# A feed forward in one unit: Strassen's product in both projections, and the samples as a stream of their own

## The chip, the core and the metric

The kernel runs on one core of one Trainium2 chip. The metric is the time of one execution on the device in microseconds (us), lower is better. The engines run side by side and wait for one another by semaphores: PE (TensorE) multiplies matrices, DVE (VectorE), ACT (ScalarE) and POOL (GpSimd) work on elements, and SP (SyncE) issues the transfers between the chip's memory (DRAM) and the core's own memory (SBUF). A matmul's result is in PSUM, a small memory of eight banks.

## What is computed

One layer of a streaming encoder in fp32, for 1024 tokens of a prompt and 8 samples of 16 tokens. These are nine tiles of 128 tokens, of 1024 features each.

```python
z = x @ w_in                         # recurrence (HGRN2) and sliding window attention
x = LN(ALPHA * x + concat(A, B) @ w_out)
x = LN(ALPHA * x + memory_attention(x) @ w_mo)
x = LN(ALPHA * x + (silu(x @ w_gate) * (x @ w_up)) @ w_down)    # d_ff = 2816
```

The last line is the feed forward, of which the change speaks. In the kernel `w_f1` holds gate and up weights and `w_f2` the down weights, both laid out in advance in the blocks that the kernel loads.

## The kernel before

An exact fp32 product is expensive on PE. So most operands are split in two parts in a faster format (`split`, L132 and L133): ACT casts the upper part `w_hi`, and DVE subtracts it from the source to get the remainder `w_lo`. A product is then three matmuls (hi·hi, lo·hi, hi·lo), `mm3`. All matmuls of a line L93 come from one helper, transposes from L97; in the changed kernel these are L95 and L99, and `split` is L137 and L138. The group column of the profile therefore names the tiles.

Two stages precede the feed forward. Stage 1 (`phase1`) projects the inputs and does both kinds of attention; its last work is the memory's keys and values (`mem_kv`), whose results go to the output and to a scratch by way of the tile `kv_sb`. Stage 2 takes the tokens in three groups of three tiles: output projection (`w_out`), layer norm, memory attention, and its projection (`mem_out`, weights `w_mo`). The rows that leave it are stored to `x2_scratch` (`x_scratch` in the profile). The samples' tile is the third of the nine.

The feed forward before runs in two units, of four and of five tiles; the samples are in the first one.

- `unit_operands` transposes a unit's rows and forms the seven operands `B11`, `T1`, `T2`, `B22`, `T3`, `B21`, `T4` of Strassen's product in Winograd's form (on ACT, POOL and DVE), each split in two.
- `hidden` makes two feature tiles, a pair, of which there are 11: it loads four weight tiles, forms the sums `s1` to `s4` on POOL and DVE, and does seven products instead of eight, each 2 × 4 × 3 matmuls, with 256 columns in the first unit and 320 in the second. Then follow tanh and two products for the gate, and the split of `h`.
- `ffn` takes a few pairs (a part), then their second projection (`proj_rows`, 512 columns, plain, three matmuls per product), and adds the result to the rows (`add_rows`, L705). With the last part come layer norm and the store.

The order on each engine comes from streams of emission, ranked, with an estimated clock (`Order`), and each engine runs its list in that order. All loads stand in one list on SP. A load stands there until its buffer is free, and all that is behind it in the list waits with it. Raw weights have three buffers (`raw_tile`), split weights four pairs.

Of the kernel before, what the change touches and what calls it, by code (L numbers as in the profile page):

```python
# [35 lines left out]
# tokens go in the order of ORDER: two tiles of the prompt, the samples (tile 8), the other tiles of the prompt  # L36
# [6 lines left out]
class Event:  # L43
    """a point on TensorE's clock from which a result is expected to be there"""
# [34 lines left out]
class TensorE:  # L79
    """TensorE with the products' cost added to the clock of an Order"""  # L80
# [19 lines left out]
def trunk(ctx, tc, I, O):  # L100
# [10 lines left out]
    wp = pool("wp")  # L111
# [6 lines left out]
    def bank(name):  # L118
        return pp[name][0].tile([P, 512], F32, name=name, bufs=pp[name][1])
# [41 lines left out]
    class Quads(list):  # L161
        """feature-major blocks [P, GW] in two parts, four to a slot"""
# [40 lines left out]
    def fm(wsrc, x, which="a", n=GW, w=None):  # L203
        """one block of columns, feature major"""
# [9 lines left out]
    ident = const.tile([P, P], F32, name="ident")  # L214
    make_identity(nc, ident)
    tri = const.tile([P, 640], U8, name="tri")
    own = const.tile([P, 8], F32, name="own")
    sinks = const.tile([P, 8], F32, name="sinks")
    sinks_s = const.tile([P, 2], F32, name="sinks_s")
    gnorm = const.tile([P, P], F32, name="gnorm")  # L220
# [3 lines left out]
    carry = const.tile([P, HGH, P], F32, name="carry")  # L224
    V.memset(carry, 0.0)
    starts = [const.tile([P, GW], F32, name=f"starts{i}") for i in range(2)]
# [142 lines left out]
    def hgrn(g, h, xt, tm):  # L369
# [53 lines left out]
        def body():  # L423
# [14 lines left out]
            # from chunks to pairs of chunks  # L438
# [45 lines left out]
    def hgrn_sample(h, qg, kdt, v, at, pl, po, sv):  # L484
        """the sample's tile: a chunk and a state for each of its sequences"""
# [25 lines left out]
    def finish(sb, mx, sk, nk):  # L511
        """rows of sb [P, n, .]: exp(s - max), normalised with the sink's share"""
# [12 lines left out]
    def swa_tile(p1, ip, t, pos, q, ak, av):  # L525
        """heads 2 ip and 2 ip + 1 of both groups, one tile of queries over its own and the preceding tile of keys"""
# [105 lines left out]
    def proj_rows(src, wsrc, evac, which, ahead=(), nt=GT, by_tile=False):  # L632
        """rows of nt tiles; src: blocks [P, nt * P] in two parts"""
# [205 lines left out]
    def mem_sample(p2, qf, ot, ready):  # L839
# [5 lines left out]
        def cache():  # L845
            """the next part of the caches, four sequences to a tile"""
# [55 lines left out]
    class Unit:  # L902
        def __init__(self, t0, nt, pieces, tmp, row, th):
            self.t0, self.nt, self.n = t0, nt, nt * 64
            self.pieces, self.tmp, self.row, self.th = pieces, tmp, row, th
            self.ready = Event()

        def operand(self, op, kt):
            for k0, hi, lo in self.pieces[op]:
                if k0 <= kt < k0 + hi.shape[1]:  # L910
                    return hi[:, kt - k0], lo[:, kt - k0]

    def unit_operands(u):
# [6 lines left out]
        for t in range(u.nt):  # L920
            b = {}
            for q in range(2):
# [4 lines left out]
                for e in range(2):  # L927
                    b[f"B{q + 1}{e + 1}"] = v[:, :, e]
# [215 lines left out]
    def wait(e):  # L1144
        yield e
# [114 lines left out]
```

## Time and profile before

| what | us |
|---|---|
| three runs | 1668.59, 1675.08, 1677.58 |
| median | 1675.08 |
| span of the profiled execution | 1669.8 |
| PE, busy | 1618.8 (97%) |
| DVE, busy | 1235.5 (74%) |
| ACT, busy | 735.8 (44%) |
| POOL, busy | 244.2 (15%) |
| DMA, mean rate | 140 GB/s |

The profile is of one execution, of which the profiler gives the span. A row of a timeline has the start in us from the span's start, the duration, the engine (SPq is SP's queue of transfers), the line, the operation, the tiles as out<-in, the count, and in brackets the idle time before it with what ended it. A row of a group ends with the count, the busy time, the mean duration of one in ns, the idle time before, and what it waited for. A DMA row has the count, the size of one, and the median time from issue to landing. Matmuls are pipelined, so their pitch, from one start to the next, is what counts, and not the duration of one.

### The profile page before, as it was taken

The page shows a single profiled execution, that of the slowest core. Times are in us where ns is not written, and L with a number is a line of the kernel's source. Part 1 is how long each engine was busy: PE and PEld are TensorE (multiplying, and loading weights), DVE is VectorE, ACT ScalarE, POOL GpSimd, SP SyncE. Part 2 cuts the span into 40 slices and gives each one's busy share as a digit, 9 for nine tenths or more (in the row PEclk, how much of TensorE's full clock was granted, in tenths as well). Part 3 has the DMA queues.
Part 4 walks back from the last instruction along what each step waited for, and adds up shares of the span by engine and source line. Part 5 has one row for each costly group of instructions (what it writes and reads, how often), then busy time and mean ns, then how long its engine had stood idle before and what let it go on. Part 6 is the DMA issues. An engine that isn't in the chain of part 4 may idle for free. (4 is left out here: it accounts for less than half of the span.)

```text
span 1669.8 us, 26720 instructions
## 1 busy us (share of the span) xinstructions
PE 1618.8 (97%) x10341; PEld 1477.3 (88%) x10341; DVE 1235.5 (74%) x2161; ACT 735.8 (44%) x1471; POOL 244.2 (15%) x234
## 2 busy tenths in 40 slices
PE   8999999999999999999988999999989999999998
PEld 7998999999878987879878898989888999989896
DVE  6887688788568666787799577667898757566568
ACT  4543455445543555224645244345543424334241
POOL 1111121111000000000232110212232111111111
PEclk9999999999999999999999999999999999999999
DMA  7453343333884588646332523132543313131231
GB/s 244 128 179 125 93 151 102 105 115 108 277 313 149 169 274 311 234 138 227 101 114 91 176 89 127 64 101 91 175 168 122 101 58 107 51 101 64 89 100 65
DMA packets 84800, 233.65 MB, mean 140 GB/s; under 512 B 10048, under 2 KB 28352, under 8 KB 84672
## 3 DMA queue, kind: packets, MB, share of 16 engines
q1 hardware_dynamic: 84672, 231.93, 42.4%
q8 instruction: 81, 1.33, 0.3%
q14 instruction: 47, 0.39, 0.1%
HBM read 210.86 MB, written 20.97 MB: 139 GB/s over the span
## 5 line engine op out<-in xcount | busy, mean ns | idle before, releaser
L133 DVE TENSOR_TENSOR w_lo<-w_raw,w_hi 128x1024 fp32r<-128x1024 f32 (+1 forms) x279 | 343.1, 1232 | 166.4 <-ACT w_hi L132 165.5
L132 ACT CAST w_hi<-w_raw 128x1024 fp32r<-128x1024 f32 (+1 forms) x279 | 290.0, 1041 | 323.8 <-PE a L93 147.0
L93 PE MATMUL a<-w_hi,h 128*128 128x512 f32 x756 | 242.6, 394 | 5.2 <-DVE rows L705 2.6
L93 PE MATMUL a<-w_hi,q_hi 128*128 128x256 f32 (+1 forms) x576 | 197.0, 344 | 3.5 <-ACT w_hi L132 2.9
L93 PE MATMUL a<-w_lo,q_hi 128*128 128x256 f32 (+1 forms) x576 | 197.0, 342 | 1.9 <-DVE w_lo L133 1.8
L93 PE MATMUL a<-w_hi,q_lo 128*128 128x256 f32 (+1 forms) x576 | 195.4, 339 | 0.0
L93 PE MATMUL a<-q_hi,w_hi 128*128 128x384 f32 x528 | 186.8, 354 | 6.8 <-ACT q_hi L132 4.3
L93 PE MATMUL a<-q_hi,w_lo 128*128 128x384 f32 x528 | 180.1, 341 | 0.0
L93 PE MATMUL a<-q_lo,w_hi 128*128 128x384 f32 x528 | 179.9, 341 | 0.0
L93 PEld LDWEIGHTS a<-w_hi,h 128*128 128x128 f32 x756 | 141.8, 188 | 38.5 <-ACT h L1000 3.6
L132 ACT CAST w_hi<-w_s 128x1024 fp32r<-128x1024 f32 x88 | 92.2, 1048 | 181.3 <-PE a L93 87.9
L133 DVE TENSOR_TENSOR w_lo<-w_s,w_hi 128x1024 fp32r<-128x1024 f32 x88 | 134.6, 1533 | 35.9 <-ACT w_hi L132 35.9
L93 PE MATMUL a<-w_lo,h 128*128 128x512 f32 x378 | 148.2, 392 | 0.0
L970 POOL TENSOR_TENSOR w_s<-w_raw 128x1024 f32<-128x1024 f32 x22 | 54.8, 2492 | 490.6 <-DMA w_raw<-in_w_f_dram 428.7
L93 PE MATMUL a<-x,w_hi 128*128 128x256 f32 x704 | 126.3, 280 | 0.0
L93 PEld LDWEIGHTS a<-w_hi,q_hi 128*128 128x128 f32 x576 | 108.5, 188 | 17.9 <-ACT w_hi L132 3.3
L705 DVE SCALAR_TENSOR_TENSOR rows<-rows,a 128x512 f32<-128x512 f32 x123 | 82.7, 682 | 55.6 <-PE a L93 55.4
L93 PEld LDWEIGHTS a<-w_lo,q_hi 128*128 128x128 f32 x576 | 108.6, 189 | 16.8 <-DVE w_lo L133 3.4
L93 PEld LDWEIGHTS a<-w_hi,q_lo 128*128 128x128 f32 x576 | 108.6, 188 | 12.7 <-issue 0.5
L93 PEld LDWEIGHTS a<-q_hi,w_hi 128*128 128x128 f32 x528 | 100.6, 191 | 11.7 <-ACT q_hi L132 4.4
L93 PEld LDWEIGHTS a<-x,w_hi 128*128 128x128 f32 x704 | 108.1, 188 | 0.3
L93 PEld LDWEIGHTS a<-q_lo,w_hi 128*128 128x128 f32 x528 | 100.8, 191 | 1.9 <-issue 0.9
(247 smaller groups left out, 3662.5 us busy)
## 6 DMA issues: line engine op xcount, KB each, us to landing
w_raw<-in_w_f_dram SPq DMA_DIRECT2D x110, 512.0 KB, 3.6
w_raw<-in_w_fm_dram SPq DMA_DIRECT2D x41, 512.0 KB, 4.1
w_raw<-in_w_tm_dram SPq DMA_DIRECT2D x24, 512.0 KB, 3.6
w_raw<-in_w_out_dram SPq DMA_DIRECT2D x24, 512.0 KB, 5.4
w_raw<-in_w_mq_dram SPq DMA_DIRECT2D x24, 512.0 KB, 4.4
w_raw<-in_w_mo_dram SPq DMA_DIRECT2D x24, 512.0 KB, 4.1
w_s<-in_w_f_dram SPq DMA_DIRECT2D x22, 512.0 KB, 4.4
ln_gb<-in_ln_dram SPq DMA_DIRECT2D x16, 512.0 KB, 6.7
```

Of the source, the lines that this page charges most:

```text
L93: return self.eng.matmul(out, lhsT, rhs, **kw)
L132: S.copy(hi, src)
L133: V.tensor_tensor(lo, src, hi.bitcast(F32), op=ALU.subtract)
L705: V.scalar_tensor_tensor(y[t][:, hs], y[t][:, hs], scale, ps, op0=ALU.mult, op1=ALU.add)
L970: G.tensor_tensor(s1, a21, a22, op=ALU.add)
```

## The change

The prompt's eight tiles are now one unit. Every hidden product has 512 columns, so each weight of `w_f1` is loaded and split once instead of twice. `h` is not kept but stored to `h_scratch` in DRAM.

The second projection now uses Strassen's product too (`second_projection`): 4 blocks of two tiles, 11 pairs in parts of 3, 3, 3 and 2. For a part, `prepare` loads `w_f2`, forms the sums of weights on POOL and splits all four tiles per pair; `inputs` loads `h` of one block, forms its sums on POOL and splits seven operands; `block` does the seven products.

The samples' first projection (`sample_hidden`) is no longer part of a unit: it multiplies plain fp32, unsplit weights `w_s` with `xs`, the transposed samples, in 22 half steps of 16 matmuls, as the stream `filler` of the lowest rank. Each half step needs two tiles of `w_f1`, so that these weights are loaded a second time. The products of the samples' second projection stand among those of the parts.

The pools of SBUF are cut anew: constants of stage 1 and the stage's right side are closed when they are done, and the feed forward opens `c` (operands), `f1` (hidden) and `f2` (second projection) in their place.

The diff, cut to what the text speaks of:

```diff
-UNITS = ((0, 4, ((0, 6), (6, 12), (12, 16), (16, 22))),
-         (4, 5, ((0, 2), (2, 6), (6, 10), (10, 14), (14, 18), (18, 22))))
+TILES = (0, 1, 3, 4, 5, 6, 7, 8)
+SAMPLE = 2
+PAIRS = FT // 2
+PARTS = ((0, 3), (3, 6), (6, 9), (9, 11))
...
+    def sample_hidden(i):
+        ps = bank("b")
+        for e in range(2):
+            w = []
+            for q in range(2):
+                w.append(ff["sample_w"]())
+                nc.sync.dma_start(out=w[q], in_=I["w_f1"][i, e * 2 + q])
+            for z in range(2):
+                for kt in range(KT):
+                    T.matmul(ps[:, cols(e * 2 + z)], w[kt // 4][:, cols(z * 4 + kt % 4)], xs[:, kt],
+                             start=kt == 0, stop=kt == KT - 1)
+            if e == 0:
+                yield
...
+        a11, a21, a22, a12 = wt("a11", 0), wt("a21", 2), wt("a22", 3), wt("a12", 1)
+        s1, s2, s4 = wt("s1"), wt("s2"), wt("s4")
+        G.tensor_tensor(s1, a21, a22, op=ALU.add)
+        G.tensor_tensor(s2, s1, a11, op=ALU.subtract)
+        G.tensor_tensor(a21, a11, a21, op=ALU.subtract)
+        G.tensor_tensor(s4, a12, s2, op=ALU.subtract)
...
+        def prepare(i):
+            w0, w1, s12, s34 = (f2.tile([P, 1024], F32, name=x, tag="w", bufs=5) for x in ("w0", "w1", "s12", "s34"))
+            for n, t in enumerate((w0, w1)):
+                nc.sync.dma_start(out=t, in_=I["w_f2"][n, i])
...
+            for t, x in ((w0, "w0"), (s12, "s12"), (s34, "s34"), (w1, "w1")):
+                out.append(parts_of(t, *(f2.tile([P, 1024], F32R, name=x + y, bufs=3) for y in "hl")))
...
+    def feed_forward(rows):
+        right.close()
...
+        ff["sample_w"] = raw_tile
...
+        order.add(all_operands(ops, rows, ready), 6)
+        order.add(filler(), 10)
+        yield ready
+        left.close()
...
+        for i in range(PAIRS):
+            yield from hidden(f1, ops, i)
+        cs.close()
+        fs.close()
+        psums.close()
...
+        ff["sample_w"] = lambda: f2.tile([P, 1024], F32, name="w_s", tag="w", bufs=5)
+        yield from second_projection(f2)
```

Three places of the order show what moved. In its rows, `[waits ...]` names the engines or queues whose semaphores the row waits for (DMAHW for earlier transfers), and xN counts equal rows.

**SP, where stage 1 ends.** Before, the first load for the output projection, `w_raw` from `w_out`, stood ahead of the stores of the last memory values:

```order
L143 DMA w_raw_5704<-in_w_mv_dram 128x1024 [waits DMAHW6_49,DVE_49]
L143 DMA w_raw_5751<-in_w_out_dram 128x1024 [waits DMAHW1_49,DVE_49]
L199 DMA raw_5640<-mix_scratch 128x384 [waits DMAHW7_49,DMAHW2_49,DVE_49]
L199 DMA raw_5644<-mix_scratch 128x384 [waits DMAHW3_49,DMAHW0_49,DVE_49]
L264 DMA out_2_dram<-kv_sb_5602 128x512 [waits Activation_49]
L266 DMA mem_kv_scratch<-kv_sb_5602 128x256 x2
L264 DMA out_2_dram<-kv_sb_5607 128x512 [waits DMAHW4_49,Activation_49]
```

Now the tiles of stage 2 and its constants come first, then the stores of the last values, which wait for ACT's copies, and behind them the first `w_out` load:

```order
L719 DMA rows_5795<-in_xtok_dram 128x1024 [waits DMAHW0_49,PE_49]
L689 DMA ln_gb_5823<-in_ln_dram 128x1024 [waits DMAHW1_49,PE_49]
L689 DMA ln_gb_5825<-in_ln_dram 128x1024 [waits DMAHW2_49]
L269 DMA out_2_dram<-kv_sb_5725 128x512 [waits DMAHW3_49,Activation_49]
L271 DMA mem_kv_scratch<-kv_sb_5725 128x256 [waits DMAHW4_49]
L271 DMA mem_kv_scratch<-kv_sb_5725 128x256 [waits DMAHW5_49]
L269 DMA out_2_dram<-kv_sb_5730 128x512 [waits DMAHW6_49,Activation_49]
L271 DMA mem_kv_scratch<-kv_sb_5730 128x256 [waits DMAHW7_49]
L271 DMA mem_kv_scratch<-kv_sb_5730 128x256 [waits DMAHW0_49]
L148 DMA w_raw_5763<-in_w_out_dram 128x1024 [waits DMAHW1_49]
```

What moved is the first `w_out` load, to a place behind two waits for ACT.

**PE, where stage 2 ends.** Before, the last product of `mem_out` (with `q`, the attention's output) was followed by the first hidden product (`x2`, the operand `B11`):

```order
L93 MATMUL a_9578<-w_hi_9520,q_lo_8637 128x512
L93 MATMUL a_9578<-w_hi_9520,q_hi_8636 128x512
L93 MATMUL a_9578<-w_lo_9521,q_hi_8636 128x512
L93 MATMUL a_9578<-w_hi_9520,q_lo_8637 128x512
L93 MATMUL a_9625<-x2_9109,w_hi_9621 128x256 [waits Activation_49]
L93 MATMUL a_9625<-x2_9110,w_hi_9621 128x256
```

Now there are 19 half steps of the samples in between, with the transposes of the eight tiles. Here is a half step with its first wait for a load, and the begin of the next one (`w_raw` is a raw tile of `w_f1`, `x2_row` a tile's rows):

```order
L95 MATMUL b_9589<-xs_5743,w_raw_9590 128x128 [waits DMAHW5_49]
L95 MATMUL b_9589<-xs_5743,w_raw_9590 128x128 x3
L95 MATMUL b_9589<-xs_5743,w_raw_9592 128x128 [waits DMAHW6_49]
L95 MATMUL b_9589<-xs_5743,w_raw_9592 128x128 x3
L95 MATMUL b_9589<-xs_5743,w_raw_9590 128x128 x4
L95 MATMUL b_9589<-xs_5743,w_raw_9592 128x128 x4
L95 MATMUL b_9589<-xs_5743,w_raw_9612 128x128 [waits DMAHW7_49]
L95 MATMUL b_9589<-xs_5743,w_raw_9612 128x128 x3
L99 MATMUL b_9638<-ident_73,x2_row_9610 128x128 [waits DMAHW1_49,PE_49,Activation_49]
L99 MATMUL b_9638<-ident_73,x2_row_9610 128x128 x3
```

What moved in is a stream that waits for a transfer every few matmuls.

**SP, where hidden ends.** Before, the `w_f2` loads of a part stood right behind, and among, those of the `w_f1` weights:

```order
L946 DMA w_raw_10134<-in_w_f1_dram 128x1024 [waits DMAHW7_49,DMAHW0_49,Pool_49]
L946 DMA w_raw_10136<-in_w_f1_dram 128x1024 [waits DVE_49]
L946 DMA w_raw_10138<-in_w_f1_dram 128x1024 [waits DMAHW3_49,DMAHW1_49,DVE_49]
L946 DMA w_s_10141<-in_w_f1_dram 128x1024 [waits DMAHW2_49]
L143 DMA w_raw_10391<-in_w_f2_dram 128x1024 [waits DMAHW0_49,Pool_49]
L143 DMA w_raw_10421<-in_w_f2_dram 128x1024 [waits DMAHW4_49,DVE_49]
L143 DMA w_raw_10451<-in_w_f2_dram 128x1024 [waits DMAHW5_49,DMAHW1_49,DVE_49]
L143 DMA w_raw_10485<-in_w_f2_dram 128x1024 [waits DMAHW6_49,DMAHW3_49,DVE_49]
L143 DMA w_raw_10491<-in_w_f2_dram 128x1024 [waits DMAHW7_49,DMAHW4_49,DVE_49]
```

Now all `w_f2` loads stand behind the last store of `h` (`th`), and the tiles for three half steps of the samples, `w_s`, behind those of the whole part and the rows `y`:

```order
L1040 DMA h_scratch<-th_12900 128x4x128 [waits DMAHW1_49]
L1040 DMA h_scratch<-th_12901 128x4x128 [waits DMAHW2_49,DVE_49]
L1040 DMA h_scratch<-th_12901 128x4x128 [waits DMAHW3_49,DVE_49]
L1083 DMA w0_12955<-in_w_f2_dram 128x1024 [waits DMAHW4_49,Activation_49,Pool_49]
L1083 DMA w1_12956<-in_w_f2_dram 128x1024 [waits DMAHW5_49]
L1106 DMA hq_13041<-h_scratch 128x1536 [waits DMAHW6_49,PE_49]
L1083 DMA w0_12981<-in_w_f2_dram 128x1024 [waits DMAHW7_49,Activation_49]
L1083 DMA w1_12982<-in_w_f2_dram 128x1024 [waits DMAHW0_49,DMAHW4_49,DVE_49,Pool_49]
L1055 DMA y_13033<-x2_scratch 64x1024 [waits DMAHW1_49]
```

Between these rows and the next ones stand the other loads of part 0 and of `y`; then, still on SP, the tiles of the samples follow:

```order
L1055 DMA y_13040<-x2_scratch 64x1024 [waits DMAHW1_49]
L1055 DMA y_13040<-x2_scratch 64x1024 [waits DMAHW2_49]
L957 DMA w_s_13092<-in_w_f1_dram 128x1024 [waits DMAHW3_49,DVE_49]
L957 DMA w_s_13094<-in_w_f1_dram 128x1024 [waits DMAHW4_49,DVE_49,Pool_49]
L957 DMA w_s_13118<-in_w_f1_dram 128x1024 [waits DMAHW5_49,DVE_49]
L957 DMA w_s_13120<-in_w_f1_dram 128x1024 [waits DMAHW6_49,DVE_49]
L957 DMA w_s_13138<-in_w_f1_dram 128x1024 [waits DMAHW7_49,DVE_49]
L957 DMA w_s_13140<-in_w_f1_dram 128x1024 [waits DMAHW3_49,DMAHW0_49,PE_49]
```

What moved is both groups of loads, to behind the end of hidden. `w_s` takes its buffers from the same ring of five as `w0`, `w1` and the sums, which is why it waits for DVE and POOL. On PE these 48 matmuls stand between the last hidden product and the first of the second projection.

More of the change, by code (lines that the diff above doesn't have):

```diff
@@ L223, in trunk @@
     V.memset(mhalf, -0.5)
[L224 removed]
+    carry = cp.tile([P, HGH, P], F32, name="carry")
     V.memset(carry, 0.0)
[L226 removed]
+    starts = [cp.tile([P, GW], F32, name=f"starts{i}") for i in range(2)]
     for t in starts:
@@ new lines, in all_operands @@
+    def all_operands(ops, rows, ready):
+        for j in range(8):
+            if j < 5:
+                row = big("x2_row")
+                nc.sync.dma_start(out=row, in_=x2_dram[TILES[j]])
+            else:
+                row = rows[j - 5]
+            yield 4000.0 if j == 0 else 2000.0
+            operands(ops, j, row)
+            yield 2500.0
+        order.set(ready, 4500.0)
+    def sample_hidden(i):
+        ps = bank("b")
+        for e in range(2):
+            w = []
+            for q in range(2):
+                w.append(ff["sample_w"]())
[6 more added lines that the diff above has]
+                yield
+        g = ps.rearrange("p (e z t) -> p e z t", e=2, z=2)
+        h = ff["sample_h"]().rearrange("p (e t) -> p e t", e=2)
+        S.activation(h, g[:, :, 0], AF.Tanh, scale=0.5)
+        V.scalar_tensor_tensor(h, h, 1.0, g[:, :, 0], op0=ALU.add, op1=ALU.mult)
+        V.scalar_tensor_tensor(h, h, 0.5, g[:, :, 1], op0=ALU.mult, op1=ALU.mult)
+        nc.sync.dma_start(out=hs_dram[:, i], in_=h)
@@ L952, in hidden, with product @@
         X, Z, W = [], [], []
-        m0, m1 = ([u.tmp("m") for _ in range(2)] for _ in range(2))
-        def product(bk, which, w_src, op, start):
-            hi, lo = (wp.tile([P, 1024], F32R, name=x, bufs=N_W) for x in ("w_hi", "w_lo"))
-            split(w_src, hi, lo)
+        def product(bk, which, w, op, start):
+            pair = parts_of(w, *(f1.tile([P, 1024], F32R, name=x, bufs=3) for x in ("w_hi", "w_lo")))
             for z in range(2):
```

381 lines of the change are left out of this document (239 added, 142 removed).

## The prediction

> **What bounds the kernel now.** I read the page's totals and its chain, then one window over the feed forward with the waits of PE in it, then the rows that give a price.
>
> ```profile
> span 1669.8 us, 26720 instructions
> PE 1618.8 (97%) x10341; PEld 1477.3 (88%) x10341; DVE 1235.5 (74%) x2161; ACT 735.8 (44%) x1471; POOL 244.2 (15%) x234
> PE 31%; DVE 6%; POOL 1%; DMA 1%; issue 1%; ACT 1%; DVEq 0%; SPq 0%; POOLq 0%
> 858.45:1661.63 803.18, 778.54 (x4925) 721.49 (x4923) 586.61 (x702) 331.13 (x505) 138.50 (x78) 0.99 0.31 102
> PE b L93 <- DVE w_lo L133: 16.4, 11, 4.2
> 858.45 0.40 PE L93 MATMUL a<-x,w_hi 128*128 128x256 f32 x2
> 1661.23 0.40 PE L93 MATMUL a<-w_hi,h 128*128 128x512 f32 x1
> ```
>
> PE is busy for 97% of the span and leads the chain with 31%, DVE following with 6%. The feed forward reaches from its first matmul at 858.45 to the end of its last at 1661.63. The window row (length, then busy time of PE, PEld, DVE, ACT, POOL) gives PE 778.5 of these 803.2 us: about 25 us of idle, 16.4 of them for DVE's `w_lo`. So this stage can gain by less PE work or by those 25 us, and it loses whatever new waits the change puts between matmuls. Behind it lies an 8.2 us tail that both kernels have in the same form.
>
> **PE's work.** Four pairs of rows give the pitch, start to start:
>
> ```profile
> 837.30 0.40 PE L93 MATMUL a<-w_hi,q_lo 128*128 128x512 f32 x1
> ...
> 840.80 0.40 PE L93 MATMUL a<-w_hi,q_lo 128*128 128x512 f32 x1
> 863.58 0.40 PE L93 MATMUL b<-x,w_hi 128*128 128x256 f32 x2
> ...
> 864.65 0.40 PE L93 MATMUL b<-x,w_hi 128*128 128x256 f32 x2
> 1352.22 0.31 PE L93 MATMUL a<-B_h,w_hi 128*128 128x320 f32 x1
> ...
> 1353.11 0.31 PE L93 MATMUL a<-B_h,w_hi 128*128 128x320 f32 x1
> 48.41 0.38 PE L93 MATMUL b<-hg_b 128*128 128x128 f32 x2
> ...
> 49.30 0.28 PE L93 MATMUL b<-hg_b 128*128 128x128 f32 x1
> 812.97 1.03 PE L97 MATMUL b<-ident,rows 128*128 128x128 f32 x8
> ```
>
> 512 columns: 15 matmuls in 3.50 us, 0.233 each. 256: nine in 1.07 (the x2 rows hold two), 0.119. 320: six in 0.89, 0.148. Plain fp32 of 128 columns (each two instructions, so x2): four in 0.89, 0.2225. A transpose: 1.03 / 8 = 0.13.
>
> Removed: hidden 1848 × 0.119 + 1848 × 0.148 = 493.4, second projection 1188 × 0.233 = 276.8; together 770. Added: hidden 7 products × 24 matmuls × 11 pairs = 1848 × 0.233 = 430.6; the prompt's second projection, 4 blocks × 7 products × 11 pairs × 3 = 924, and the sample's, 132, so 1056 × 0.233 = 246.0; the sample's first projection 352 × 0.2225 = 78.3. Together 755. PE saves 15 us; with pitches between 0.230 and 0.237 this moves by 10 either way. Everything else is waits.
>
> **Ahead of the feed forward.** The first `w_out` load stood ahead of the last memory-value stores; now it stands behind them, three row loads and two `ln` loads.
>
> ```profile
> 448.95 0.33 SPq L143 DMA_DIRECT2D w_raw<-in_w_out_dram  x1
> 461.89 0.49 PE L93 MATMUL a<-w_hi,q_hi 128*128 128x512 f32 x1 [0.68 <-ACT kv_sb L263]
> 463.02 1.12 SPq L266 DMA_DIRECT2D mem_kv_scratch<-kv_sb  x2
> w_raw<-in_w_out_dram SPq DMA_DIRECT2D x24, 512.0 KB, 5.4
> L132 ACT CAST w_hi<-w_raw 128x1024 fp32r<-128x1024 f32 x109 | 114.5, 1051 | 116.5 <-PE a L93 60.5 <-PE b L93 41.0 <-issue 11.0
> 844.07 0.75 PE L93 MATMUL a<-w_hi,q_hi 128*128 128x512 f32 x2 [2.87 <-ACT w_hi L132]
> 847.85 0.50 PE L93 MATMUL a<-w_lo,q_hi 128*128 128x512 f32 x1 [1.39 <-DVE w_lo L133]
> ```
>
> PE's row at 461.89 is its first `w_out` matmul. Before, that load was issued at 448.95, and PE had hardly to wait. Now it can leave after the store that was issued from 463.02 to 464.14, lands 5.4 us later, and the cast takes 1.05: 470.6, or 8.7 later; with some matmuls at a slow clock (below) I take +9.5 (7 with a landing of 3.6, 12 at most). On the other side the first unit's operands leave `mem_out`: its two waits of 2.87 and 1.39 and 32 transposes (4.2) go, 8 transposes for the sample (1.0) come: −7.4. The feed forward starts at 860.6.
>
> **The filling stream.** 19 of the sample's 22 half steps stand ahead of the first hidden product. Each is 16 matmuls, 3.56 us, over two raw tiles of a ring of three. A half step's second tile takes the buffer of the previous one's first, which is free after its twelfth matmul; so from one such tile's landing to the next lie 8 matmuls (1.78), about 0.2 for a semaphore, and a load's issue to landing.
>
> ```profile
> w_raw<-in_w_f_dram SPq DMA_DIRECT2D x110, 512.0 KB, 3.6
> w_s<-in_w_f_dram SPq DMA_DIRECT2D x22, 512.0 KB, 4.4
> raw<-in_memT_dram SPq DMA_DIRECT2D x8, 128.0 KB, 2.5
> L933 POOL TENSOR_TENSOR tt<-stage 128x256 f32<-128x256 f32 x10 | 9.4, 951 | 32.2 <-ACT stage L925 32.2
> L933 POOL TENSOR_TENSOR tt<-stage,tt 128x256 f32<-128x256 f32 x10 | 8.2, 818 | 0.4
> ```
>
> At 3.6 the period is 5.6 and the fill takes 19 × 5.6 = 106 us, where its matmuls need 68. The ends: 2.5, which a quarter of the bytes took, gives 85; 4.4 gives 121. The Trainium skill ("DMA: Bandwidth & Descriptors", Anatomy of one DMA) has 2.0 us plus bytes at 436 GB/s, by its figures an estimate of 3.2 for this load and 98 for the fill; the measured 3.6 stays. The transposes fall into PE's waits. The operands' own chain per tile (four POOL subtractions of 0.8 to 0.95, casts and remainders beside them, about 6 us) fits into the 11 us of a pair, so it is hidden by the loads; were these faster, it would hide up to 8 × 6 = 48. The first hidden weights wait for the last raw tile: 0.33 + 3.6 + 1.05 and a remainder of 1.25, less four matmuls, is 5, with the slow clock 6.5. Hidden starts at 973.
>
> **Hidden.** 430.6. Per pair PE needs 39 us; DVE's seven remainders and its adds about 17, POOL's four products 10 (rows below): no bound, even in turn. I add 2: 1406.
>
> **From hidden to second projection.** The new rows of the order put all this behind the last product, whose end is E.
>
> ```profile
> 1042.40 2.40 POOL L970 TENSOR_TENSOR w_s<-w_raw 128x1024 f32<-128x1024 f32 x1 [36.68 <-DMA w_raw<-in_w_f_dram]
> 1042.93 2.95 DVE L133 TENSOR_TENSOR w_lo<-w_raw,w_hi 128x1024 fp32r<-128x1024 f32 x1 [0.40 <-ACT w_hi L132]
> L970 POOL TENSOR_TENSOR w_s<-w_raw 128x1024 f32<-128x1024 f32 x21 | 52.3, 2489 | 490.6 <-DMA w_raw<-in_w_f_dram 428.7 <-DVE rows L705 36.1 <-ACT w_hi L132 25.7
> L133 DVE TENSOR_TENSOR w_lo<-w_raw,w_hi 128x1024 fp32r<-128x1024 f32 x110 | 138.1, 1255 | 57.5 <-ACT w_hi L132 57.3
> L133 DVE TENSOR_TENSOR q_lo<-raw,q_hi 128x384 fp32r<-128x384 f32 x40 | 21.5, 562 | 2.5 <-ACT q_hi L132 2.4
> L705 DVE SCALAR_TENSOR_TENSOR rows<-rows,a 128x512 f32<-128x512 f32 x88 | 59.0, 683 | 41.4 <-PE a L93 41.3
> ```
>
> The last store of h leaves after a 0.7 us DVE step; only then the first `w_f2` loads are issued, landing at E + 5.5. Then part 0 is prepared: 12 DVE remainders of 1.255 and 7 of 0.56, 19 us; on POOL 12 products of 512 columns, estimated at 1.42 between the 0.88 of 256 and the 2.49 of 1024, and 4 of 384 at 1.15: 21.6. The two rows at 1042 show them in turn: DVE's 2.95 instead of 1.255 ends 1.08 after POOL's end. In turn they need 40.6: E + 46. The sample's last three half steps come next on PE, but their tiles take the buffers of this preparation; the last but one leaves at its end, so the last half step ends at E + 46 + 0.3 + 3.6 + 3.6 = E + 53, and second-projection matmuls stand behind it. Of that 10.7 is work: 42 idle. If POOL and DVE ran freely, POOL's 21.6 with one more uncovered landing, cast and remainder would give 30. I take 40, nearer the rows' turn; ends 27 and 42. The Trainium skill ("SBUF — State Buffer", two separate sides) says the pair's port is an exclusive lock for a whole instruction; by that the sum has 42, without it 30, and the rows agree with the lock.
>
> **Second projection.** 246.0, and three boundaries of parts. Four split tiles per pair in rings of three are all held by the running part, so the next part's third pair goes after the last product: cast 1.05, remainder 1.25, load 3.9, three POOL products 4.3 in turn with two remainders 2.5, cast 1.05: 14, against 37 matmuls that can be placed ahead, 8.6; 5.4 idle.
>
> ```profile
> 862.00:870.00 8.00, 6.34 (x54) 6.14 (x53) 8.00 (x7) 5.27 (x10) 2.19 (x1) 1.00 0.21 66
> 1003.00:1010.00 7.00, 3.77 (x20) 3.57 (x19) 7.00 (x7) 3.13 (x8) 2.68 (x1) 0.77 0.22 77
> 867.06 0.39 PE L93 MATMUL a<-x,w_lo 128*128 128x256 f32 x1 [1.66 <-DVE w_lo L133]
> 1006.85 0.58 PE L93 MATMUL b<-x,w_lo 128*128 128x256 f32 x1 [3.23 <-DVE w_lo L133]
> 1010.36 0.40 PE L93 MATMUL b<-x,w_hi 128*128 128x256 f32 x2
> ```
>
> The granted clock (the number after POOL's) was 0.77 where PE had waited 3.23 us (16 matmuls in 3.51 instead of 1.90, so 1.6 lost) and 1.00 around a wait of 1.66. So a boundary costs 7, the last, of a two-pair part, 3: 17 (0 to 30).
>
> **Sum.** 1406 + 40 + 10.7 + 246 + 17 + 8.2 = 1727.9 of span. The median of the runs, 1675.1, lies 5.3 above the profiled span: 1733. Of the 58 us more, fill waits are 38, the two starts 9, the transition 40, boundaries 17, against 15 of PE work, the 25 of old idle and 7 ahead.
>
> **Rivals.** (1) The second projection is bound by DVE and POOL in turn: 44 remainders of 1.255, 112 smaller ones (59), POOL's 44 × 1.42 and 64 smaller (69) are 246, of which 40 are counted; the rest with 112 adds of 0.683 is 282 against 263: +19, 1752. For it the rows at 1042; against it, adds read PSUM and can run beside POOL. (2) The clock falls in the fill too: matmuls at 0.445 make the period 7.4 and the time 1767. It speaks for it that PE will be 64% busy there; against it that waits of 1.7 left 1.00. The Trainium skill's page "TensorE: Matmul & The Clock Gate" (HAM oscillation) describes just this for short bursts between DMA waits. (3) The fill does fill: loads are ahead of PE, and its 38 us go: 1695. Against it stands the ring. (4) On the other side: loads land faster than the groups say. Some 28 landings follow one another on the path (19 in the fill, 1 ahead of hidden, 4 in the transition, 3 at boundaries, 1 of `w_out`); each microsecond less is 28. At 1.6 us instead of 3.6 the time is 1677, as before; below 1.3 it is faster, at 1.0 about 1660. For it, the fill has fewer loads in flight than the groups had; against it, no row shows even 128 KB under 2.5.
>
> **Chances.** Forecast 0.54 (1705 to 1760 by its bounds), rival 1 0.09, rival 2 0.05, rival 3 0.08, rival 4 0.24, half of it faster and half near no change. A measurement can tell about 0.5%, 8 us. So faster 0.12, same 0.12, slower 0.76. The range leaves out rival 4 but for its upper end: 1680 to 1772.
>
> **What would show it.** Right: a period of 5 to 6 us and PE waiting for `w_raw` after 860, PE's busy share there near 0.64; a hole of 30 us or more after the last hidden product in which DVE and POOL alternate; holes of 5 to 7 us at three part boundaries. Wrong: fill loads in 2 us, or sample matmuls that cover the transition because the split tiles come free early, or second-projection matmuls that run before the sample's.

## The result, and the profile after

The changed kernel takes 1787.88 us (median; the kernel before, beside it on the same chip, 1675.08): ratio 1.069, 95% interval 1.0651 to 1.0729. Forecast were 1733 and a range of 1680 to 1772: slower, as forecast, but by 113 us instead of 58. One of its five executions, the profiled one, took 2086.79 us at a mean granted clock of 0.74; the ratio leaves it out, and the profile below is of another execution of the same kernel: 1786.28 us, clock 0.965.

From the page of the changed kernel, whose span is 1784.5 us:

```profile
PE 1627.9 (91%) x9065; PEld 1404.9 (79%) x9065; DVE 1137.4 (64%) x2065; ACT 663.4 (37%) x1348; POOL 389.8 (22%) x333
PE 79%; DMA 8%; DVE 5%; POOL 4%; ACT 1%; issue 1%; SPq 1%; DVEq 0%; ACTq 0%; POOLq 0%
```

PE is as busy as before (1618.8) in a span that is 115 us longer, though it was to have 15 us less work: what came is waiting, and some matmuls at a lower clock. DMA and POOL appear in the chain with 8% and 4%, where they had 1% each.

The windows by stage (length, then busy time and count of PE, PEld, DVE, ACT, POOL; granted clock, DMA share, GB/s): the filling stream, hidden, the hole behind it, the samples' last three half steps, the second projection, the tail.

```profile
858.50:966.80 108.30, 84.96 (x673) 79.40 (x671) 40.97 (x74) 31.45 (x81) 35.85 (x41) 0.97 0.62 208
970.60:1402.70 432.10, 431.54 (x1848) 349.16 (x1848) 201.90 (x208) 138.82 (x175) 109.36 (x44) 1.00 0.25 77
1402.70:1451.50 48.80, 0.02 (x1) 0.02 (x1) 28.16 (x20) 15.33 (x19) 26.93 (x16) 0.53 0.69 197
1451.50:1464.80 13.30, 13.30 (x97) 13.30 (x97) 1.60 (x3) 1.03 (x3) 1.08 (x2) 0.80 0.82 291
1464.80:1772.70 307.90, 260.02 (x1058) 206.52 (x1057) 228.88 (x323) 85.51 (x148) 131.04 (x98) 0.93 0.26 80
1772.70:1784.50 11.80, 0.00 (x0) 0.00 (x0) 7.12 (x14) 0.00 (x0) 1.91 (x2) 0.71 0.39 89
```

Beside the forecast:

| step | forecast | measured |
|---|---|---|
| start of the fill | 860.6 | 858.5 |
| fill | 106.4 | 108.3 |
| to hidden's first product | 6.5 | 3.8 |
| hidden | 432.6 | 432.1 |
| hole behind hidden | 40 | 48.8 |
| samples' last half steps | 10.7 | 13.3 |
| second projection | 263 | 307.9 |
| tail | 8.2 | 11.8 |
| span | 1727.9 | 1784.5 |

The forecast had hidden end 3.4 us later than it did, at 1406 instead of 1402.7. All that it lacks, 60 us, lies behind that: 45 in the second projection, 9 in the hole, 6 in the samples' last half steps (whose clock is 0.80) and the tail.

The waits of PE from there to the end (engine and tile that waited, what for, us in total, times, longest):

```profile
PE b L95 <- DMA w_s<-in_w_f_dram: 48.8, 1, 48.8
PE x L95 <- ACT hh L137: 14.0, 3, 6.5
PE x L95 <- DVE y L1123: 13.8, 6, 3.8
PE z L95 <- DVE y L1123: 7.3, 1, 7.3
PE z L95 <- ACT s12h L137: 5.9, 2, 3.5
PE w L95 <- DVE hl L138: 4.3, 1, 4.3
PE x L95 <- DVE w0l L138: 2.4, 3, 0.8
```

Behind the hole no wait is for a `w_f2` load. Of these 48 us, 21 are for DVE's adds (`y`), 14 for casts of `h`, 8 for split weights (`s12h`, `w0l`) and 4 for a remainder of `h` (`hl`). The windows by part (columns as above) tell where:

```profile
1464.80:1537.00 72.20, 68.84 (x302) 55.95 (x302) 47.88 (x68) 21.87 (x39) 30.11 (x23) 1.00 0.24 77
1537.00:1621.00 84.00, 72.21 (x293) 57.46 (x292) 62.17 (x72) 27.31 (x43) 42.83 (x30) 0.94 0.24 80
1621.00:1703.00 82.00, 71.25 (x291) 56.93 (x289) 60.02 (x73) 26.53 (x43) 40.81 (x29) 0.94 0.23 73
1703.00:1772.70 69.70, 47.72 (x178) 36.18 (x176) 58.81 (x113) 9.79 (x23) 17.29 (x19) 0.85 0.34 91
```

PE's work is 288 × 0.233 = 67.1 in a part of three pairs and 192 × 0.233 = 44.7 in the last one. So the parts lose 5.1, 16.9, 14.9 and 25.0: 62 in all, where the forecast had 17 for three boundaries. (The windows hold 302, 293, 291 and 178 matmuls, not exactly a part each, so up to 3 us of these losses belong to a neighbour.) Not all of the 62 is idle time: PE is busy for 260.0 us with matmuls that were put at 246, at a granted clock of 0.93, so 14 are slower matmuls and 48 are waits.

22 of the 48 lie at the three boundaries: 8.1, 7.0 and 7.2. At the second part's begin PE waits 0.85 for a split weight, then 3.75 for the first cast of `h` and 3.46 for a split sum:

```profile
1541.96 0.61 PE L95 MATMUL x<-w0h,hh 128*128 128x512 f32 x1 [3.75 <-ACT hh L137]
1552.10 0.53 PE L95 MATMUL z<-s12h,hh 128*128 128x512 f32 x1 [3.46 <-ACT s12h L137]
```

The other 25 lie inside the parts: one wait each in the first three (2.52, 3.78 and 3.78, all for an add) and 15 in the last one.

The second part shows how a wait inside comes about. DVE, POOL and PE in the same 10 us (a row of a timeline as before; DVE first, then POOL, then PE):

```profile
1557.36 3.21 DVE L138 TENSOR_TENSOR hl<-ht,hh 128x384 fp32r<-128x384 f32 x2
1560.50 3.64 DVE L138 TENSOR_TENSOR hl<-hq,hh 128x384 fp32r<-128x384 f32 x3
1564.53 0.67 DVE L1123 SCALAR_TENSOR_TENSOR y<-y,x 128x512 f32<-128x512 f32 x1
1558.56 1.60 POOL L1088 TENSOR_TENSOR s<-w,w 128x512 f32<-128x512 f32 x1
1565.26 0.50 PE L95 MATMUL x<-s34h,hh 128*128 128x512 f32 x1 [3.78 <-DVE y L1123]
```

DVE has two, then three remainders of `h`, of 0.55 each when alone (a row of the next run), and needs 3.21 and 3.64 for them, because POOL forms sums of weights at the same time. The add of `x` stands behind them in DVE's list and starts at 1564.53; PE has been standing since 1561.48 for the PSUM bank that this add empties, until 1565.26.

### The profile page after: what moved, and what is told of

It reads as the page before. It is cut to its first block, busy times and chain, and to the rows that moved or that the text cites. A ratio compares the mean times of both kernels' runs of the same rounds, so it can differ in the third digit from the quotient of the medians.

```text
span 2085.0 us, 24292 instructions
## 1 busy us (share of the span) xinstructions
PE 1957.2 (94%) x9065; PEld 1546.0 (74%) x9065; DVE 1138.1 (55%) x2065; ACT 666.1 (32%) x1348; POOL 383.2 (18%) x333
## 4 chain that ended last, share of the span: by engine, by line
PE 87%; DMA 5%; POOL 3%; DVE 2%; issue 1%; ACT 1%; SPq 1%; DVEq 0%; POOLq 0%; ACTq 0%
PE a L95 51%; PE b L95 23%; PE x L95 6%; PE z L95 3%; PE b L99 3%; DMA w_raw<-in_w_f_dram 3%; PE s L95 2%; PE w L95 1%; DVE hl L138 1%; POOL s L1086 1%; POOL s L1087 1%; DMA w<-in_w_f_dram 1%; POOL s L1088 1%; DMA w_s<-in_w_f_dram 0%; POOL s L1089 0%
## 5 line engine op out<-in xcount | busy, mean ns | idle before, releaser
L138 DVE TENSOR_TENSOR w_lo<-w_raw,w_hi 128x1024 fp32r<-128x1024 f32 (+1 forms) x169 | 204.3, 1211 | 159.8 <-ACT w_hi L137 159.4
L137 ACT CAST w_hi<-w_raw 128x1024 fp32r<-128x1024 f32 (+1 forms) x169 | 174.4, 1033 | 263.8 <-PE a L95 155.0
L138 DVE TENSOR_TENSOR w_lo<-a,w_hi 128x1024 fp32r<-128x1024 f32 x44 | 56.0, 1273 | 125.6 <-ACT w_hi L137 124.1
L95 PE MATMUL a<-T_l,w_hi 128*128 128x512 f32 x264 | 120.5, 457 | 0.0
L95 PE MATMUL a<-T_h,w_lo 128*128 128x512 f32 x264 | 120.5, 456 | 0.0
L95 PE MATMUL a<-T_h,w_hi 128*128 128x512 f32 x264 | 120.4, 456 | 0.0
L95 PEld LDWEIGHTS a<-q_hi,w_lo 128*128 128x128 f32 x528 | 106.1, 201 | 9.2 <-DVE w_lo L138 0.4
L95 PE MATMUL b<-xs,w_raw 128*128 128x128 f32 x608 | 91.0, 319 | 14.2 <-DMA w_raw<-in_w_f_dram 13.8
L137 ACT CAST w_hi<-a 128x1024 fp32r<-128x1024 f32 x44 | 46.2, 1049 | 176.3 <-PE a L95 85.4
L95 PEld LDWEIGHTS b<-xs,w_raw 128*128 128x128 f32 x608 | 87.0, 231 | 18.7 <-DMA w_raw<-in_w_f_dram 18.5
```

Of the source, the lines that this page charges most:

```text
L95: return self.eng.matmul(out, lhsT, rhs, **kw)
L137: S.copy(hi, src)
L138: V.tensor_tensor(lo, src, hi.bitcast(F32), op=ALU.subtract)
```

## Experiments

Theories, as the expectations name them: W, the waits that the rows show, against C, a lower clock; T, DVE and POOL in turns; L, the loads of the filling stream; N, the layer norms in the last part; Q, the queue of loads ahead of `w_s`; D, DVE's own list; S and P, on the place of the samples. All edits are to the changed kernel, and each gain below is against its 1786.28 (one execution; the four behind the ratio lie between 1784.1 and 1796.27, so a gain of a few us is hardly clear of the noise). The start of the fill lies between 856.8 and 864.2 in these profiles, and stages that an edit does not touch differ by up to 4 us from one to the next (the second projection: 307.9, 304.8 and 303.9); so each stage is compared by its own length.

### The kernel again

> The changed kernel as it is, looked at once more. Theory W (waits): PE runs the 512-column matmuls at 0.233 us as before, so hidden takes about 432 us at a granted clock near 0.99; what is more than forecast (1787 against 1733) lies in waits, with the hole after hidden at 40 to 50 us and the second projection at 290 us or more. Theory C (clock): hidden itself takes 455 us or more at a granted clock under 0.97, and the second projection about 265 us as forecast.

Measured: 1786.28, the rows above. Hidden ran at a clock of 1.00 and 431.5 of its 432.1 us were PE's work; the loss is in the waits behind it and in the matmuls that they slow. C falls.

### The sums on DVE

```diff
-            G.tensor_tensor(s1, a21, a22, op=ALU.add)
+            V.tensor_tensor(s1, a21, a22, op=ALU.add)
... (the same for all eight sums in prepare and inputs)
```

> The second projection's sums of weights and of h (prepare and inputs) are made on DVE instead of POOL. Theory T (DVE and POOL take turns at SBUF, so a sum costs the time it takes wherever it runs): the hole after hidden becomes 8 to 12 us shorter, since a sum of 512 columns costs DVE about 0.7 us instead of 1.4, and the second projection as a whole 15 to 40 us shorter. Theory F (they run freely side by side): DVE, which has the longer list, gets 40 us more work in the second projection, the hole grows by about 8 us, and the kernel is 10 to 40 us slower than the changed kernel.

Measured: 1745.09, ratio to before 1.0438 (1.0414 to 1.0462), 41 us less. The groups of DVE's remainders from the end of hidden on (count, busy us, mean ns), of the changed kernel:

```profile
L138 DVE TENSOR_TENSOR w1l<-w,w1h 128x1024 fp32r<-128x1024 f32 x11 | 22.6, 2055 | 1.2 <-ACT w1h L137 1.2
```

and with the sums on DVE, where such a sum takes 0.68 (the last row):

```profile
L138 DVE TENSOR_TENSOR hl<-hq,hh 128x384 fp32r<-128x384 f32 x48 | 25.7, 551 | 0.0
L138 DVE TENSOR_TENSOR w1l<-w,w1h 128x1024 fp32r<-128x1024 f32 x11 | 13.4, 1216 | 0.0
L1086 DVE TENSOR_TENSOR s<-w 128x512 f32<-128x512 f32 x11 | 7.5, 682 | 0.0
```

Its parts:

```profile
1454.00:1520.00 66.00, 64.02 (x283) 52.39 (x282) 45.46 (x84) 19.47 (x38) 0.00 (x0) 1.00 0.26 87
1520.00:1590.00 70.00, 69.05 (x299) 55.33 (x299) 62.76 (x103) 29.48 (x47) 0.00 (x0) 1.00 0.29 96
1590.00:1660.00 70.00, 68.69 (x298) 54.91 (x297) 61.40 (x102) 27.71 (x45) 0.00 (x0) 1.00 0.26 85
1660.00:1732.00 72.00, 51.21 (x184) 39.10 (x183) 64.73 (x128) 8.19 (x21) 6.86 (x7) 0.81 0.33 88
```

With 94 more operations in this stage DVE is busy for 234.4 instead of 228.9 us: the remainders had contained POOL's time. The first three parts come down to 66.0, 70.0 and 70.0, next to PE's 67.1; the hole goes from 48.8 to 36.9. The last part keeps its 72. At the begin of the second and third part PE now waits 0.80 and 0.76 instead of 8.1 and 7.0. T holds. The sums themselves also got shorter (0.68 instead of 1.25 or more on POOL); how much of the 41 us that is was not separated from the turns. The Trainium skill ("SBUF — State Buffer", two separate sides) has DVE and POOL share a pair of ports by an exclusive lock; the trace agrees in that the remainder of 1.216 alone takes 2.055 beside POOL.

### Without the last layer norm

```diff
-                        final_norm(y[b, e], gb, bn[e], b, e)
+                        out_rows(O["y"], b, e, y[b, e], slice(0, 1024))
```

> The prompt's last layer norm is left out (y is stored as it is). Theory N (in the last part DVE has eight tiles' norms, about 39 us, beside adds and remainders, for 45 us of matmuls): the last part, 69.7 us in the changed kernel, falls to 48 to 55, the tail of 12 us to about 6, the whole by 18 to 28 us. Theory B (the last part waits for its weights' preparation like the others): it falls by less than 8 us, the whole by less than 14.

Measured: 1768.12, ratio 1.0566 (1.0532 to 1.06), 18 less. The second projection and its last part:

```profile
1469.00:1760.70 291.70, 257.15 (x1059) 204.06 (x1057) 207.84 (x272) 85.70 (x148) 124.46 (x93) 0.95 0.27 85
1708.40:1760.70 52.30, 43.85 (x178) 34.15 (x176) 35.72 (x62) 9.83 (x23) 11.63 (x13) 0.93 0.43 124
```

The last part falls from 69.7 to 52.3, DVE's work in it from 58.8 to 35.7, and the tail from 11.8 to 5.4. In the changed kernel the norms stand in DVE's list among the adds of the part that has least work for PE; their three main groups:

```profile
L1067 DVE SCALAR_TENSOR_TENSOR y<-y,rs,ln_gb 128x512 f32<-128x512 f32 x16 | 11.3, 745 | 0.0
L1066 DVE SCALAR_TENSOR_TENSOR y<-y,mv,ln_gb 128x512 f32<-128x512 f32 x16 | 11.2, 743 | 0.0
L1127 DVE BATCH_NORM_STATS2 bn<-y 128x6 f32<-128x512 f32 x16 | 10.6, 683 | 0.1
```

33 us. N holds; T and N together cover the 62: 37 in the first three parts, of which the sums on DVE left 5, and 25 in the last one, of which this run left 7.6. In it PE's waits of 4.35, 2.56 and 7.32 us among the last blocks are gone.

### The samples' last half steps with the others

```diff
         yield ready
+        yield from filled(PAIRS)
```

(the place: `feed_forward`, ahead of hidden; none is left behind it)

> All 22 half steps of the samples are in the filling stream ahead of hidden, none after it. Theory S (the sample tiles, which wait for part 0's preparation, hold up the second projection): the fill grows by three periods, 17 us; after hidden the second projection starts as soon as the first weights and operands are split, 30 to 36 us after the last hidden product instead of about 60, so the whole is 5 to 15 us faster than the changed kernel. Theory P (the preparation itself is the whole hole): it starts 46 us or later after hidden, and the whole is no faster than the changed kernel or slower.

Measured: 1792.57, ratio 1.0729 (1.0703 to 1.0756), 6 more. From the last hidden product to the first one of the second projection it is 15.9 us now. The second projection:

```profile
1437.30:1775.70 338.40, 272.89 (x1056) 210.15 (x1056) 251.41 (x336) 96.13 (x162) 149.31 (x111) 0.90 0.31 94
```

and two of PE's waits in it, which had been 13.8 (six times) and 5.9 (twice):

```profile
PE x L95 <- DVE y L1123: 17.2, 9, 3.5
PE z L95 <- ACT s12h L137: 13.6, 4, 4.7
```

PE starts after 16 us instead of 48.8, and the second projection then needs 338.4 instead of 307.9: 17.6 more of idle time, for part 0's split weights and the adds behind them, and 12.9 more in slower matmuls (clock 0.90). From the end of hidden to the end it is 366.1 (to 1787.5), against 368.5 (381.8 less the 13.3 of the samples, which moved ahead); the three half steps cost 16 in the fill (22 half steps in 124.5 against 19 in 108.3). So the hole was not lost time alone: part 0's preparation was in it. The second projection starts sooner than either theory had it, 16 us after hidden and not 30 to 36 or 46, but the whole is no faster, as P said: the 5 to 15 us of S did not come.

### Half of the loads in the filling stream

```diff
-            for q in range(2):
-                w.append(ff["sample_w"]())
-                nc.sync.dma_start(out=w[q], in_=I["w_f1"][i, e * 2 + q])
+            w.append(ff["sample_w"]())
+            nc.sync.dma_start(out=w[0], in_=I["w_f1"][i, e * 2])
+            w.append(w[0])
```

(each half step multiplies one tile twice, so half of the samples' weights are left out)

> Each half step of the samples loads only one of its two tiles of w_f1 and uses it twice (the other half of these weights is left out of the samples' first projection). Theory L (the fill waits for the landing of its second tile): the half step's period falls from 5.6 us to 3.6 to 4.2, and the stage ahead of hidden from 105 us to 65 to 80. Theory O (the operands' chain or PE itself holds it): the stage gets shorter by less than 10 us.

Measured: 1752.07, ratio 1.0482 (1.0465 to 1.05), 34 less, all of it in the fill:

```profile
858.60:933.70 75.10, 75.09 (x673) 74.85 (x672) 42.15 (x74) 32.32 (x81) 35.27 (x41) 1.00 0.52 168
```

PE is busy for 75.09 of 75.10 us. So 33 of the fill's 108.3 hang on the loads: 23 of idle time, and the rest in matmuls behind the waits. L holds.

### The two tiles of a half step one after the other

```diff
-            for z in range(2):
-                for kt in range(KT):
+            for q in range(2):
+                for z in range(2):
+                    for kt in range(q * 4, q * 4 + 4):
```

(all eight matmuls of the first raw tile, then those of the second, so that a buffer is free after 8 instead of 12. The groups of gate and up then alternate in one PSUM bank, which changes the samples' sums; where the edit is used again below, each has a bank.)

> A half step of the samples uses its first tile for all eight of its matmuls and then its second one, instead of changing tile every four matmuls. Theory L (the ring's period: a tile is held for most of a half step): a buffer is held for 1.8 us plus 0.2 and 3.6 for the next load, three of them in 5.6 us, so a half step takes 3.7 us instead of 5.7, and the stage ahead of hidden falls from 112 us to 75 to 85; the whole by 25 to 35. Theory R (the rate of the transfers or SP's list holds it): less than 10 us.

Measured: 1766.69, ratio 1.0575 (1.0557 to 1.0593), 20 less:

```profile
864.20:952.30 88.10, 80.42 (x673) 76.14 (x671) 40.44 (x74) 31.85 (x81) 36.20 (x41) 1.00 0.79 258
```

88.1 instead of 108.3, with the same loads, at 258 instead of 208 GB/s: it was the order of the matmuls that kept the buffers. This lies above the 75 to 85 that was expected: 7.7 us of idle time remain, and PE is busy for 80.4 with what took 75.1 where loads did not bind.

### The rows of blocks 1 to 3 later

```diff
-        for b in range(4):
-            for e in range(2):
-                out_rows(x2_dram, b, e, y[b, e], None)
+        for e in range(2):
+            out_rows(x2_dram, 0, e, y[0, e], None)
...
+                if n == 0 and b < 3:
+                    for e in range(2):
+                        out_rows(x2_dram, b + 1, e, y[b + 1, e], None)
```

> The rows y of the last three blocks (12 of 16 loads) are loaded ahead of their block instead of ahead of the samples' last tiles. Theory Q (the queue sets the hole's end: the first sample tile is issued after the 14 y loads at 1442.5 and lands 9 us later, behind them): the samples' matmuls start 8 to 13 us earlier, and the end of the kernel comes 6 to 13 us earlier. Theory D (DVE and POOL, in turn, set the end of everything after hidden): the samples start earlier, but the second projection takes as much longer, and the whole changes by less than 4 us.

Measured: 1781.54, ratio 1.066 (1.0638 to 1.0683), 5 less. The hole in the changed kernel, where SPq is the list of loads:

```profile
1409.63 1.23 DVE L138 TENSOR_TENSOR w0l<-w,w0h 128x1024 fp32r<-128x1024 f32 x1 [6.24 <-ACT w0h L137]
1409.89 2.09 POOL L1086 TENSOR_TENSOR s<-w 128x512 f32<-128x512 f32 x1 [63.93 <-DMA w<-in_w_f_dram]
1410.85 2.20 DVE L138 TENSOR_TENSOR w1l<-w,w1h 128x1024 fp32r<-128x1024 f32 x1
1411.94 2.24 POOL L1088 TENSOR_TENSOR s<-w,w 128x512 f32<-128x512 f32 x1
1414.14 1.25 POOL L1087 TENSOR_TENSOR s<-s,w 128x512 f32<-128x512 f32 x1
1430.84 10.92 SPq L1055 DMA_DIRECT2D y<-x_scratch  x14
1442.49 14.84 SPq L957 DMA_DIRECT2D w_s<-in_w_f_dram  x6
1451.48 0.80 PE L95 MATMUL b<-xs,w_s 128*128 128x128 f32 x2 [48.82 <-DMA w_s<-in_w_f_dram]
```

and in this one:

```profile
1436.24 16.61 SPq L957 DMA_DIRECT2D w_s<-in_w_f_dram  x6
1441.30 1.78 PEld L95 LDWEIGHTS b<-xs,w_s 128*128 128x128 f32 x8 [34.96 <-DMA w_s<-in_w_f_dram]
```

In the changed kernel the 14 loads of `y` take 10.92 us to leave, and the first `w_s` leaves behind them, at 1442.49, when part 0's preparation is all but done (1443.57). It lands 9.0 us later. Here it leaves 30 us after the end of hidden instead of 40 and lands after 5.1. The samples start 14 us sooner after hidden, wait once more for 5.3, and the second projection starts 54.4 us after hidden's end instead of 62.1. From hidden's end to the end of the kernel it is 371.8 instead of 381.8: 10 of the 14 reach the end in this execution, with hidden ending 4 later. The 5 us of the time lie near the noise and between what Q (6 to 13) and D (under 4) expected, so the rows show that the queue held the samples up, and how much of it the kernel's time gains stays open.

### A short part first

```diff
-PARTS = ((0, 3), (3, 6), (6, 9), (9, 11))
+PARTS = ((0, 2), (2, 5), (5, 8), (8, 11))
```

> The parts are of 2, 3, 3 and 3 pairs instead of 3, 3, 3 and 2. Theory D (preparation on DVE and POOL in turn is the hole, and norms overload the last part): the first preparation is a third shorter, so the hole falls by 8 to 14 us, and the last part has 67 us of matmuls for its norms, so that its idle 25 us fall to 10 to 15; the whole by 12 to 25 us. Theory Q (the y loads set the hole): the hole stays within 3 us and the whole falls by 5 to 12.

Measured: 1771.82, ratio 1.0609 (1.0579 to 1.064), 14 less. Its second projection:

```profile
1453.50:1759.00 305.50, 262.34 (x1058) 206.30 (x1057) 238.76 (x323) 88.61 (x148) 138.61 (x100) 0.94 0.27 85
```

The hole is 35.6, since a part of two pairs is prepared sooner. The second projection does not pay for it: PE's waits inside the first part grow from 2.5 to 8.0, and those inside the last one, where the norms now stand beside three pairs, fall from 15.1 to 9.7. D's 12 to 25 hold, nearly all of it in the hole.

### These edits together

The sums on DVE, the rows later, the half steps tile by tile (gate and up in a bank each) and the short part first.

> Four edits at once: sums of the second projection on DVE, rows y late, the samples' half steps tile by tile (each half of gate and up in a PSUM bank of its own, so that nothing is left out), parts of 2, 3, 3 and 3. If the effects lay in places of their own they would add up: 42 + 8 + 20 + 15 us, 1701. Since three of them shorten the same hole after hidden (from 49 to 37, 35 and 36 one by one), theory D (one list of DVE work sets everything after hidden) gives less: 1705 to 1725, with the hole at 15 to 25 and the last part still waiting for DVE.

Measured: 1706.07, ratio 1.0193 (1.0169 to 1.0217). Hole and second projection:

```profile
1387.60:1406.00 18.40, 0.13 (x1) 0.13 (x1) 12.34 (x16) 8.41 (x11) 0.00 (x0) 0.60 0.89 268
1420.10:1692.70 272.60, 252.87 (x1059) 200.08 (x1057) 241.99 (x422) 89.25 (x152) 6.87 (x7) 0.97 0.36 109
```

The four alone had lowered the ratio by 0.0252, 0.003, 0.0115 and 0.0081, 0.048 in all; together it is 0.050. So in the whole time the effects add up, within a noise of some 5 us for each, and they are some 80 of the 113 us. By stages they do not: the hole falls by 30, where one by one it fell by 12, 14 and 13. The time, at the lower end of D's 1705 to 1725 and 5 above the 1701 of plain addition, does not decide between them; the hole, 18.4, is as D had it.

### The second projection without Strassen's product

```diff
-            G.tensor_tensor(s1, a21, a22, op=ALU.add)
... (no sums; two split tiles per pair, four operands per block)
+            for n, (which, e, half) in enumerate((("x", 0, 0), ("z", 0, 1), ("x", 1, 0), ("w", 1, 1))):
+                ps = product(which, half, e)
+                add(b, e, half, ps, st(e))
```

> One part undone: the prompt's second projection by plain products, 1056 matmuls instead of 924 (31 us more on PE at 0.233), without the sums of weights and of h, with 22 instead of 44 split weight tiles, 64 instead of 112 split operands and 64 instead of 112 adds. Theory D (DVE and POOL set this stage): in spite of 31 us more PE work the time after hidden falls, from 382 to 325 to 350 us, the whole to 1730 to 1755. Theory P (PE's matmuls set it): the whole rises by 15 to 30.

Measured: 1737.24, ratio 1.0378 (1.0351 to 1.0405), 49 less, with 132 matmuls more. Its second projection:

```profile
1457.90:1727.50 269.60, 269.60 (x1191) 222.90 (x1189) 126.29 (x218) 47.97 (x87) 7.78 (x8) 1.00 0.30 92
```

PE is busy for 269.60 of 269.60 us; its only wait behind hidden is the hole, with 35.8 us 13 shorter than in the changed kernel. DVE's work there falls from 228.9 to 126.3. The second projection's own Strassen product, as it is built here, thus costs 307.9 − 269.6 = 38 us; its saving of 132 matmuls was bought with DVE and POOL work that nothing covers. D holds.

### The plain second projection with the other edits

> The edits of e9 with the plain second projection, its split weights in rings of six in the room of the sums, so that the next part can be prepared while one runs. Theory D: PE is the bound again after hidden: a hole of 10 to 20 us, then 1056 + 132 matmuls, 277 us, and 10 to 15 of waits in the last part; 1700 to 1720, no slower than e9. If PE's 31 us count in full it is 1725 or more.

Measured: 1699.11, ratio 1.0152 (1.0129 to 1.0175), the best of all, and still 1.5% slower than before. Its fill:

```profile
862.50:952.50 90.00, 81.13 (x673) 76.43 (x671) 39.84 (x74) 31.98 (x81) 36.47 (x41) 1.00 0.79 255
```

In a span of 1698.9 against 1669.8 the fill has 90.0, 15 above the 75.1 without waits for loads, and the hole still takes 17.5. These two are 32 of PE's waits, more than the 25 of idle time in the whole feed forward before. Nor has PE less to do in this form: its busy time is 1639.3 against 1618.8. By the prediction's own prices hidden saves 493.4 − 430.6 = 63 us, and the samples' first projection in plain fp32 costs 78.

## Why the prediction was wrong, point by point

**The step that failed is the second projection's waits.** Their only term was the boundaries of parts, "a boundary costs 7, the last, of a two-pair part, 3: 17 (0 to 30)". Measured 62. The boundaries themselves were not far off: 22 of idle time, though more of it for casts of `h` (14.0) than for the split weights (8.3) that were forecast. What was put at nothing are the 25 us of waits inside the parts; and the lower clock behind all these waits took 14, where 1.6 a boundary had been allowed. Two things were missing.

The first is rival 1, DVE and POOL in turn over the whole stage. It had the right mechanism, as the sums on DVE show, which left 5 of the 37 us in the first three parts, and the wrong price, +19. That price sums up the work of both engines and sets it against PE's total. But DVE works through its list in order, and a burst of late remainders delays the adds behind it, which free PSUM banks; PE stands although DVE has idle time elsewhere (228.9 busy of 307.9). Such a sum is a lower bound only. The argument against it, that adds can run beside POOL, is beside the point: they stand behind remainders that can't.

The second is a cost that was in no term: the norms of eight tiles, 33 us of DVE in three groups, in the part with 44.7 us of PE work. The prediction took the tail as "in the same form" and did not ask what DVE had to do while the last blocks ran. Without the norm, 16 us of the second projection and 6 of the tail go.

**The hole**, 40 forecast, 48.8 measured. Part 0's preparation ended 41 us after hidden, forecast 46, so the turns of the rows at 1042 were priced about right. What was mis-sized is the last term, "E + 46 + 0.3 + 3.6 + 3.6": it let the first half steps run during the preparation and only the last one wait for its end. The 14 loads of `y` ahead of all `w_s` were not counted, though the order's rows show the last of them there; the first `w_s` left 40 us after hidden and took 9.0 to land.

**Right**: the start (858.5 against 860.6; PE waits 8.40 for the first `w_out` weights, at 470.05, where 8.7 had been worked out), the fill's period (108.3 / 19 = 5.70 against 5.6), and hidden (0.2338 a matmul). **Luck**: the start, the fill, the step to hidden and hidden itself came within 3.4 us in all partly because errors of 2 to 3 us go both ways. The 38 us that were called the fill's waits are 33: the transposes, which were to fall into PE's waits, are part of the 75.1 us that PE needs without these. The list that splits the 58 us into terms does not add up from its own figures either: the old feed forward has 803.2 − 770 = 33 us beside its matmuls, not 25. The sum of the time does not rest on that list.

**The rivals**: rival 2 is out by its price, since the fill's period stayed at 5.70 and not 7.4; its mechanism is there in small. Over the fill the clock is 0.97: it fell twice, behind waits of 2.35 us (ending at 933.71) and 2.69 (at 946.90), where 32 matmul instructions took 5.47 us instead of 3.84; it did not fall behind one of 2.46 (at 904.93).

The Trainium skill ("TensorE: Matmul & The Clock Gate", HAM oscillation) has the clock fall when PE idles for longer than a window of about 3.4 us. The hole, 48.8, with its 0.53 agrees; the two waits in the fill were shorter, so here that length is no safe bound. Rival 3 is out: the ring bound the loads, as the tile-by-tile order showed. Rival 4 is out: the fill's loads took 4.0 in the median (the row's last number) and not 1.6,

```profile
w_raw<-in_w_f_dram SPq DMA_DIRECT2D x38, 512.0 KB, 4.0
```

although it held 0.24 of the chances, with every row against it. The range ended at 1772, just above rival 2's 1767: it took in one rival's cost at a time and never two together.

## What to carry to other kernels

When a change saves matmuls by sums on other engines, set those engines' lists, not their totals, against PE block by block: what stands ahead of the operation that empties a PSUM bank is on the path. Elementwise work given to POOL is not free while DVE has a list of remainders; here that was 41 us, and taking it back cost DVE 5.5 us of busy time in the second projection. Look at the last part separately, for it has the least matmuls and the norms, and count every load on the queue ahead of the one that PE waits for, the cheap ones too.

## What was not expected of the hardware

A load of 512 KB took 9.0 us from issue to the matmul that it released where 14 loads of 256 KB had been issued in the 11 us before it, against 5.1 without these. POOL is slowed by DVE as DVE by POOL: its sum of 512 columns took 2.24 beside DVE's remainder at 1411.94, and 1.25 at 1414.14, when DVE was idle. The rows at 1409.63 to 1414.14 show turns and not a shared rate: DVE's first remainder takes 1.23, its time alone, and each of the next three instructions ends 1.1 us after the other engine's last one. DVE's adds from PSUM keep their time beside POOL: 0.681 us in the mean, as with the sums on DVE (0.682). The plain second projection ran at 269.6 / 1188 = 0.227 us for a matmul of 512 columns, where hidden has 0.234 for the same shape; why was not tried.
